# A Conformer/Hyena block on one NeuronCore: short convolutions in the tokens' own order, pieces turned by ScalarE, and the last group's LayerNorm laid beside its last short convolution

## The chip, the core and the metric

The kernel runs on one core of a Trainium2 chip. The metric is the time of one execution on the device, in microseconds; the kernel before takes 2048.83 us (median of three runs, 2046.94 to 2049.76). The engines are PE (TensorE, matrix products), DVE (VectorE), ACT (ScalarE), POOL (GpSimd; here it issues some transfers) and SP, which issues most transfers. Each works through its own instructions in order. "Column" below means 128 of the 7168 output channels of the input projection.

## What is computed

One encoder layer on 2048 tokens of width 1024 in float32: an RMSNorm, one input projection to 7168 channels, two mixers, and an output projection. The channels of both mixers come in eight groups of 128.

```python
p = einsum('bld,de->ble', rmsnorm(x), w_in)
c_val, c_gate, c_z, hy_p, hy_z = split(p)
a = c_val * sigmoid(c_gate)
a = depthwise_conv_centred(a, conf_dw_w)                 # width 31: 31 taps
a = silu(group_layernorm(a)) * silu(c_z)                 # 8 groups
hp = depthwise_conv_centred(hy_p, hy_short_w)            # width 3
x0, x1, v = split(hp)
y = bidir_fftconv(v * x1, h_fwd, h_bwd, hy_skip) * x0    # as a two-step transform
y = group_rmsnorm(y) * silu(hy_z)
out = rmsnorm(x + concat([a, y]) @ w_out)
```

## The kernel before

A column of the projection is computed in four *chunks* of 512 tokens (`chunk`, lines 242 to 251): for each of the eight 128-row blocks of the input three 512-wide matmuls (lines 246 to 248, since both operands are split into a high and a low part), so 24 matmuls a chunk. The result `mm` lies in one of four PSUM buffers until ACT or DVE has taken it. `fetch` (233 to 240) loads a column's weights and splits them: the high part `wh` by ACT (237), the low part `wl` by DVE (239). `wh` and `wl` have two buffers each, the raw `wr` one.

The middle of the kernel (from 340 us to 1465 us of the span) is a loop over the eight groups (694 to 735). In pass `i`:

- `conf_glu` forms gate times value of group `i` in `apad`, and the LayerNorm of group `i-1` (`conf_norm`) goes on meanwhile: ACT and DVE split each chunk of the sum `acc` (556, 557), two matmuls subtract the mean over the channels (562, 563), ACT squares and copies (564, 565), and four small matmuls form the variances (569). Then root, reciprocal (571, 572) and `stacked` (227 to 229).
- `conf_taps` adds the 31 taps of the width-31 convolution: each is one pass over 2048 tokens on DVE (541). It is a generator; `some(n)` issues the next `n` taps at the place in the program where it stands, so that DVE gets them between other work.
- `conf_tail` scales, gates and stores group `i-1` (584 to 590).
- `hz_gate` (only for `i` below 7) computes the gate's column.
- `hyena(i-1)`: `x1_out` and `gated` compute two columns; each chunk goes to `ppad` (608, ACT) and through `short_conv`: ACT multiplies by the middle weight (619), DVE adds the other two (621, 622). In `x1_out` the output is written *turned*: token 32 a + b lands at column 64 b + a of the tile (`turned`, 592 to 594), the order in which the transform wants it, so neighbours in time lie 64 elements apart. In `gated` the convolution is in the tokens' order, and DVE multiplies it into the turned tile (640).
- `stage1(i-1)`, the transform's first step, runs beside the chunks of `x0_out` (two of its steps in each chunk): PE transposes 512 columns of the gated tile (662), ACT takes the result (664), PE multiplies (679), ACT takes that (682) and SP stores it to `AU`. Transposes, products and the LayerNorm's matmuls share three PSUM buffers named `aux`.
- `x0_out` computes the third column, also turned (619, 621, 622), and `some(99)` issues all taps that are left.

After the loop come the three columns of group 7, with its LayerNorm and tail written between `hyena(7)` and `x0_out(7)`, the loads of the output weights (`wo_load`, by POOL) and their splits (`wo_split`), and the last gate's column (`hz_gate(7)`). Then the output projection starts (784 to 786) beside the transform's second step.

The program is not executed in exactly the order in which it is written: a scheduler puts each engine's instructions in order by the place in the program and by when it takes their inputs to be ready. The orders shown below are those that it put out.

The functions that the diff touches:

Of the kernel before, what the change touches and what calls it, by code (L numbers as in the profile page):

```python
# [13 lines left out]
AF = mybir.ActivationFunctionType  # L14
# [5 lines left out]
L = 2048  # L20
# [3 lines left out]
TC = 512  # L24
# [157 lines left out]
def hybrid_kernel(ctx: ExitStack, tc: tile.TileContext, A, out):  # L182
# [283 lines left out]
    def long(dt=F32):  # L466
        return wk.tile([P, L], dt, name="long", bufs=3)
# [30 lines left out]
    with ExitStack() as c0:  # L498
# [43 lines left out]
                                               op0=OP.mult, op1=OP.add)  # L542
                yield

        def conf_norm(prev):


            acc, = prev
            sqs, split = long(), None
            for t in range(NT + 1):  # L550
                ready = split
                if t < NT:
# [39 lines left out]
        def turned(x):  # L592

            return x.rearrange("p (n2 n1) -> p n1 n2", n2=N2)

        def hz_gate(i, some, store=True, order=range(NT)):
            hz = long()
            for t, ts, pt in inproj(48 + i, order=order):
                nc.scalar.activation(turned(hz)[:, 16 * t:16 * (t + 1)], pt.rearrange("p (a b) -> p a b", b=N2), AF.Copy)
                some(1)  # L600
            if store:
                nc.sync.dma_start(HZ[i], hz)
            return hz
# [6 lines left out]
                    after(t - 1)  # L610
            after(NT - 1)

        def short_conv(co, a, j, turn=False):
            n = TC

            def v(x):
                return x.rearrange("p (a b) -> p a b", b=N2) if turn else x

            nc.scalar.activation(co, v(ppad[:, a + 1:a + 1 + n]), AF.Identity, bias=sm("sh_b", j),  # L619
                                 scale=sm("sh_w", 3 * j + 1))  # L620
            nc.vector.scalar_tensor_tensor(co, v(ppad[:, a:a + n]), sm("sh_w", 3 * j), co, op0=OP.mult, op1=OP.add)  # L621
            nc.vector.scalar_tensor_tensor(co, v(ppad[:, a + 2:a + 2 + n]), sm("sh_w", 3 * j + 2), co,  # L622
                                           op0=OP.mult, op1=OP.add)

        def x1_out(i, some):
            s = long()

            def conv(t):
                short_conv(turned(s)[:, 16 * t:16 * (t + 1)], t * TC, 8 + i, turn=True)
                some(1)  # L630

            short_in(32 + i, after=conv)
            return s

        def gated(s, i, some):
            def conv(t):
                c = tmp()
                short_conv(c, t * TC, 16 + i)
                to = turned(s)[:, 16 * t:16 * (t + 1)]
                nc.vector.tensor_mul(to, to, c.rearrange("p (a b) -> p a b", b=N2))  # L640

            short_in(40 + i, after=conv)

        def x0_out(i, some, side, store=True):
            c = long()

            def conv(t):
                short_conv(turned(c)[:, 16 * t:16 * (t + 1)], t * TC, i, turn=True)
                some(1)

            short_in(24 + i, side, after=conv)
            if store:
                nc.sync.dma_start(X0[i], c)
            return c

        def stage1(i, s, some):
            def turn(q):
# [27 lines left out]
                yield  # L685

        def hyena(i, some):
            s = x1_out(i, some)
            gated(s, i, some)
            some(HY)  # L690
            return stage1(i, s, some)

        prev = side = None
        for i in range(NG):
# [22 lines left out]
            if i:  # L717
                side = hyena(i - 1, some)
                x0_out(i - 1, some, side)
            some(99)  # L720
        for _ in side:
            pass
        side = hyena(NG - 1, some)
        for _ in conf_norm(prev):
            pass
        wo_load(0, 0)
        conf_tail(NG - 1, *prev, lambda n: None)
        wo_split(0, 0, apad_tile(F32R))
        x0 = x0_out(NG - 1, lambda n: None, side, store=False)
        wo_load(0, 1, wp.tile([P, D], F32, name="wr", bufs=1))  # L730
        wo_load(0, 2, wp.tile([P, D], F32, name="wh"))
        wo_load(0, 3, wp.tile([P, D], F32, name="wl"))
# [375 lines left out]
```

## Time and profile before

| | us |
|---|---|
| median of three runs | 2048.83 |
| the profiled execution, whole | 2048.57 |
| its span, first to last instruction | 2046.8 |
| PE busy | 1981.5 (97%) |
| DVE busy | 1486.7 (73%) |
| ACT busy | 1046.6 (51%) |
| POOL busy | 44.2 (2%) |

The span is 1.8 us shorter than the execution. Matmuls are pipelined: each row of a 512-wide matmul has 0.39 us, but one starts every 0.23 us, so PE's busy time hides gaps shorter than a row. The granted clock is 1.00 where PE runs at its upper level (2.4 GHz) and 0.5 at its lower one (1.2 GHz).

### The profile page before, as it was taken

The page shows a single profiled execution, that of the slowest core. Times are in us where ns is not written, and L with a number is a line of the kernel's source. Part 1 is how long each engine was busy: PE and PEld are TensorE (multiplying, and loading weights), DVE is VectorE, ACT ScalarE, POOL GpSimd, SP SyncE. Part 2 cuts the span into 40 slices and gives each one's busy share as a digit, 9 for nine tenths or more (in the row PEclk, how much of TensorE's full clock was granted, in tenths as well). Part 3 has the DMA queues.
Part 4 walks back from the last instruction along what each step waited for, and adds up shares of the span by engine and source line. Part 5 has one row for each costly group of instructions (what it writes and reads, how often), then busy time and mean ns, then how long its engine had stood idle before and what let it go on. Part 6 is the DMA issues. An engine that isn't in the chain of part 4 may idle for free.

```text
span 2046.8 us, 23642 instructions
## 1 busy us (share of the span) xinstructions
PE 1981.5 (97%) x9304; PEld 1456.5 (71%) x9304; DVE 1486.7 (73%) x1339; ACT 1046.6 (51%) x1410; POOL 44.2 (2%) x90
## 2 busy tenths in 40 slices
PE   6999999999999999999999999999999999989998
PEld 4766688887787887887877877776655555556666
DVE  5587729499599599697795995997455555566774
ACT  5478711253343433433433534445677778555662
POOL 0000000000000000000000000000100000111110
PEclk9999999999999999999999999999999999999999
DMA  8524411120311212113202213121898888997862
GB/s 305 192 98 152 172 37 62 42 82 31 103 52 52 83 62 83 59 45 93 83 23 81 83 31 103 31 83 52 252 282 252 251 263 259 323 246 225 233 171 62
DMA packets 159663, 265.76 MB, mean 130 GB/s; under 512 B 12854, under 2 KB 99254, under 8 KB 155456
## 3 DMA queue, kind: packets, MB, share of 16 engines
q1 hardware_dynamic: 152448, 240.13, 38.0%
q0 software_dynamic: 7104, 24.12, 4.2%
q8 instruction: 73, 1.20, 0.3%
q14 instruction: 38, 0.31, 0.1%
HBM read 163.54 MB, written 100.66 MB: 129 GB/s over the span
## 4 chain that ended last, share of the span: by engine, by line
PE 71%; DVE 18%; issue 6%; ACT 3%; DMA 3%; POOL 0%; SPq 0%; DVEq 0%; POOLq 0%; ACTq 0%
PE mm L246 13%; PE mm L248 13%; PE mm L247 13%; DVE long L541 7%; PE o L784 6%; PE o L785 5%; PE o L786 5%; PE u L874 3%; PE k L874 3%; DVE long L622 2%; DVE long L621 2%; PE aux L679 1%; PE hp L382 1%; PE Y L971 1%; DVE t L622 1%
## 5 line engine op out<-in xcount | busy, mean ns | idle before, releaser
L246 PE MATMUL mm<-uh,wh 128*128 128x512 f32 x1792 | 710.3, 397 | 6.8 <-ACT wh L237 3.5
L248 PE MATMUL mm<-uh,wl 128*128 128x512 f32 x1792 | 702.4, 392 | 4.1 <-DVE wl L239 4.1
L247 PE MATMUL mm<-ul,wh 128*128 128x512 f32 x1792 | 702.3, 392 | 1.7 <-DVE ul L307 1.7
L541 DVE SCALAR_TENSOR_TENSOR long<-apad,small,long 128x2048 f32<-128x2048 f32 x240 | 564.5, 2352 | 8.9 <-ACT long L538 6.9
L246 PEld LDWEIGHTS mm<-uh,wh 128*128 128x128 f32 x1792 | 337.7, 189 | 107.3 <-issue 25.1
L248 PEld LDWEIGHTS mm<-uh,wl 128*128 128x128 f32 x1792 | 338.1, 189 | 78.5 <-DVE wl L239 5.1
L247 PEld LDWEIGHTS mm<-ul,wh 128*128 128x128 f32 x1792 | 338.3, 189 | 76.5 <-DVE ul L307 3.7
L608 ACT ACTIVATE ppad<-mm 128x512 f32<-128x512 f32 x96 | 57.3, 597 | 218.6 <-PE mm L248 196.6
L784 PE MATMUL o<-wo,mh 128*128 128x512 f32 x384 | 155.4, 405 | 1.5 <-ACT mh L1012 1.5
L786 PE MATMUL o<-wo,ml 128*128 128x512 f32 x384 | 152.4, 397 | 0.1
L785 PE MATMUL o<-wo,mh 128*128 128x512 f32 x384 | 152.5, 397 | 0.0
L883 ACT ACTIVATE long<-long 32x1024 f32<-32x1024 f32 x128 | 135.3, 1057 | 2.1
L237 ACT ACTIVATE wh<-wr 128x1024 fp32r<-128x1024 f32 x56 | 59.6, 1064 | 140.1 <-PE mm L247 129.8
L533 DVE TENSOR_TENSOR apad<-mm,apad 128x512 f32<-128x512 f32 x32 | 22.1, 691 | 147.4 <-PE mm L248 147.4
L889 DVE TENSOR_TENSOR long<-long,k 128x1024 f32<-128x1024 f32 x64 | 75.4, 1217 | 72.8 <-PE k L874 67.1
L784 PEld LDWEIGHTS o<-wo,mh 128*128 128x128 f32 x384 | 72.2, 188 | 46.2 <-issue 30.0
L239 DVE TENSOR_TENSOR wl<-wr,wh 128x1024 fp32r<-128x1024 f32 x56 | 68.6, 1225 | 41.7 <-ACT wh L237 41.0
L621 DVE SCALAR_TENSOR_TENSOR long<-ppad,small,long 128x512 f32<-128x512 f32 x64 | 85.8, 1343 | 6.5 <-ACT long L619 6.5
L619 ACT ACTIVATE long<-ppad,small 128x512 f32<-128x512 f32 x64 | 84.7, 1324 | 3.6 <-DMA HZ<-long 1.4
L622 DVE SCALAR_TENSOR_TENSOR long<-ppad,small,long 128x512 f32<-128x512 f32 x64 | 86.4, 1350 | 0.1
L786 PEld LDWEIGHTS o<-wo,ml 128*128 128x128 f32 x384 | 72.4, 189 | 17.5 <-issue 2.5
L785 PEld LDWEIGHTS o<-wo,mh 128*128 128x128 f32 x384 | 72.3, 188 | 17.7 <-issue 4.5
(176 smaller groups left out, 2294.5 us busy)
## 6 DMA issues: line engine op xcount, KB each, us to landing
wr<-in_w_in_dram SPq DMA_DIRECT2D x56, 512.0 KB, 3.6
AK<-ak SPq DMA_DIRECT2D x64, 256.0 KB, 2.0
AU<-t SPq DMA_DIRECT2D x64, 256.0 KB, 3.1
au<-AU SPq DMA_DIRECT2D x64, 256.0 KB, 4.3
ak<-AK SPq DMA_DIRECT2D x64, 256.0 KB, 5.2
VD<-vs SPq DMA_DIRECT2D x64, 256.0 KB, 4.4
long<-VD SPq DMA_DIRECT2D x16, 1024.0 KB, 7.5
xn<-in_x_dram SPq DMA_DIRECT2D x16, 512.0 KB, 5.7
```

Of the source, the lines that this page charges most:

```text
L246: mm(pt, wh[:, k], uh[t][:, k], start=(k == 0), stop=False)
L247: mm(pt, wh[:, k], ul[t][:, k], start=False, stop=False)
L248: mm(pt, wl[:, k], uh[t][:, k], start=False, stop=(k == KT - 1))
L541: nc.vector.scalar_tensor_tensor(acc, apad[:, j:j + L], sm("dw_w", i * CK + j), acc, op0=OP.mult, op1=OP.add)
L619: nc.scalar.activation(co, v(ppad[:, a + 1:a + 1 + n]), AF.Identity, bias=sm("sh_b", j), scale=sm("sh_w", 3 * j + 1))
L621: nc.vector.scalar_tensor_tensor(co, v(ppad[:, a:a + n]), sm("sh_w", 3 * j), co, op0=OP.mult, op1=OP.add)
L622: nc.vector.scalar_tensor_tensor(co, v(ppad[:, a + 2:a + 2 + n]), sm("sh_w", 3 * j + 2), co, op0=OP.mult, op1=OP.add)
L784: mm(o, mh[:, k], wh[:, cs], start=(k == 0), stop=False)
L785: mm(o, mh[:, k], wl[:, cs], start=False, stop=False)
L786: mm(o, ml[:, k], wh[:, cs], start=False, stop=(k == KT - 1))
L874: mm(o[rows2(k), HALF[i]], g[rows2(i), j:j + 64], x[rows2(i), HALF[k]], start=True, stop=True)
L883: nc.scalar.activation(uw[32 * q:32 * (q + 1)], us[32 * (q ^ 1):32 * (q ^ 1) + 32], AF.Copy)
```

## The change

Three things are changed.

1. `short_conv` works in the tokens' own order everywhere. Its turned accesses are gone; `turn_in` (622 to 623 in the changed file) lets ACT copy a finished piece into its turned place instead. `x1_out` turns nothing, `gated` multiplies into the small tile `c` and turns the product into a new long tile `g`, and `x0_out` turns its finished convolution. Per group that is eight turned copies on ACT more.
2. The taps of group 7 are no longer all issued before `hyena(7)`: `some(99)` stands behind it for the last group.
3. The LayerNorm of group 7 and its tail become a generator (`last_norm`) that takes one step each time `stage1(7)` takes one (`together`), that is two steps a chunk of `x0_out(7)`. Its squares lie in the tile of `apad` instead of a long one. The first load and split of output weights stand behind `x0_out(7)`.

```diff
-        def conf_norm(prev):
+        def conf_norm(prev, sqs=None):
...
-            sqs, split = long(), None
+            sqs, split = long() if sqs is None else sqs, None
...
-                nc.scalar.activation(turned(hz)[:, 16 * t:16 * (t + 1)], pt.rearrange("p (a b) -> p a b", b=N2), AF.Copy)
+                turn_in(hz, t, pt)
...
-        def short_conv(co, a, j, turn=False):
+        def short_conv(co, a, j):
             n = TC
-            def v(x):
-                return x.rearrange("p (a b) -> p a b", b=N2) if turn else x
-            nc.scalar.activation(co, v(ppad[:, a + 1:a + 1 + n]), AF.Identity, bias=sm("sh_b", j),
+            nc.scalar.activation(co, ppad[:, a + 1:a + 1 + n], AF.Identity, bias=sm("sh_b", j),
                                  scale=sm("sh_w", 3 * j + 1))
-            nc.vector.scalar_tensor_tensor(co, v(ppad[:, a:a + n]), sm("sh_w", 3 * j), co, op0=OP.mult, op1=OP.add)
-            nc.vector.scalar_tensor_tensor(co, v(ppad[:, a + 2:a + 2 + n]), sm("sh_w", 3 * j + 2), co,
+            nc.vector.scalar_tensor_tensor(co, ppad[:, a:a + n], sm("sh_w", 3 * j), co, op0=OP.mult, op1=OP.add)
+            nc.vector.scalar_tensor_tensor(co, ppad[:, a + 2:a + 2 + n], sm("sh_w", 3 * j + 2), co,
                                            op0=OP.mult, op1=OP.add)
+        def turn_in(to, t, x):
+            nc.scalar.activation(turned(to)[:, 16 * t:16 * (t + 1)], x.rearrange("p (a b) -> p a b", b=N2), AF.Copy)
 
         def x1_out(i, some):
             s = long()
             def conv(t):
-                short_conv(turned(s)[:, 16 * t:16 * (t + 1)], t * TC, 8 + i, turn=True)
+                short_conv(s[:, t * TC:(t + 1) * TC], t * TC, 8 + i)
                 some(1)
...
         def gated(s, i, some):
+            g = long()
             def conv(t):
                 c = tmp()
                 short_conv(c, t * TC, 16 + i)
-                to = turned(s)[:, 16 * t:16 * (t + 1)]
-                nc.vector.tensor_mul(to, to, c.rearrange("p (a b) -> p a b", b=N2))
+                nc.vector.tensor_mul(c, s[:, t * TC:(t + 1) * TC], c)
+                turn_in(g, t, c)
             short_in(40 + i, after=conv)
+            return g
 
         def x0_out(i, some, side, store=True):
-            c = long()
+            g = long()
             def conv(t):
-                short_conv(turned(c)[:, 16 * t:16 * (t + 1)], t * TC, i, turn=True)
+                c = tmp()
+                short_conv(c, t * TC, i)
+                turn_in(g, t, c)
                 some(1)
...
         def hyena(i, some):
-            s = x1_out(i, some)
-            gated(s, i, some)
+            s = gated(x1_out(i, some), i, some)
...
-            some(99)
+            if i < NG - 1:
+                some(99)
         for _ in side:
             pass
         side = hyena(NG - 1, some)
-        for _ in conf_norm(prev):
-            pass
+        some(99)
+
+        def last_norm():
+            yield from conf_norm(prev, apad_tile()[:, :L])
+            conf_tail(NG - 1, *prev, lambda n: None)
+            yield
+
+        def together(*steps):
+            live = list(steps)
+            while live:
+                for g in list(live):
+                    if next(g, live) is live:
+                        live.remove(g)
+                yield
+
+        side = together(last_norm(), side)
+        x0 = x0_out(NG - 1, lambda n: None, side, store=False)
         wo_load(0, 0)
-        conf_tail(NG - 1, *prev, lambda n: None)
         wo_split(0, 0, apad_tile(F32R))
-        x0 = x0_out(NG - 1, lambda n: None, side, store=False)
```

Three places of the engines' orders, before and after. In the changed file line 621 is 617, 622 is 618, 619 is 615, 640 is 641, 662 is 667, 664 is 669, 679 is 684 and 682 is 687; 623 is the turned copy.

The first is ACT, in a steady group (behind the third variance root, 571): the last piece of `gated` and the first ones of `x0_out`. Before:

```order
L237 ACTIVATE wh<-wr 128x1024
L608 ACTIVATE ppad<-mm 128x512
L619 ACTIVATE t<-ppad,small 128x512
L608 ACTIVATE ppad<-mm 128x512
L619 ACTIVATE long<-ppad,small 128x16x32
L608 ACTIVATE ppad<-mm 128x512
L619 ACTIVATE long<-ppad,small 128x16x32
L664 ACTIVATE t<-aux 128x512 x2
```

After:

```order
L237 ACTIVATE wh<-wr 128x1024
L608 ACTIVATE ppad<-mm 128x512
L615 ACTIVATE t<-ppad,small 128x512
L623 ACTIVATE long<-t 128x16x32
L608 ACTIVATE ppad<-mm 128x512
L615 ACTIVATE t<-ppad,small 128x512
L623 ACTIVATE long<-t 128x16x32
L608 ACTIVATE ppad<-mm 128x512
L623 ACTIVATE long<-t 128x16x32
L669 ACTIVATE t<-aux 128x512 x2
```

The turned copies (623) stand between the evacuation of a chunk (608) and the next; each waits for DVE's product, and the transposes' evacuation (669) stands behind the last of them.

The second is DVE in group 7, from the last taps to the LayerNorm's split (557). Before:

```order
L541 SCALAR_TENSOR_TENSOR long<-apad,small,long 128x2048
L622 SCALAR_TENSOR_TENSOR long<-ppad,small,long 128x16x32
L239 TENSOR_TENSOR wl<-wr,wh 128x1024
L621 SCALAR_TENSOR_TENSOR t<-ppad,small,t 128x512
L622 SCALAR_TENSOR_TENSOR t<-ppad,small,t 128x512
L640 TENSOR_TENSOR long<-long,t 128x16x32
L621 SCALAR_TENSOR_TENSOR t<-ppad,small,t 128x512
L622 SCALAR_TENSOR_TENSOR t<-ppad,small,t 128x512
L640 TENSOR_TENSOR long<-long,t 128x16x32
L621 SCALAR_TENSOR_TENSOR t<-ppad,small,t 128x512
L239 TENSOR_TENSOR wl<-wr,wh 128x1024
```

After:

```order
L239 TENSOR_TENSOR wl<-wr,wh 128x1024
L618 SCALAR_TENSOR_TENSOR long<-ppad,small,long 128x512
L541 SCALAR_TENSOR_TENSOR long<-apad,small,long 128x2048
L617 SCALAR_TENSOR_TENSOR t<-ppad,small,t 128x512
L541 SCALAR_TENSOR_TENSOR long<-apad,small,long 128x2048
L618 SCALAR_TENSOR_TENSOR t<-ppad,small,t 128x512
L641 TENSOR_TENSOR t<-long,t 128x512
L617 SCALAR_TENSOR_TENSOR t<-ppad,small,t 128x512
L618 SCALAR_TENSOR_TENSOR t<-ppad,small,t 128x512
L641 TENSOR_TENSOR t<-long,t 128x512
L617 SCALAR_TENSOR_TENSOR t<-ppad,small,t 128x512
L239 TENSOR_TENSOR wl<-wr,wh 128x1024
```

The first row of before is the last tap (541): it stood before all pieces of `gated`, and now the last one stands behind the first pass of the first piece. The next column's weight split (239, the second one in each) stands between two pieces, as before.

The third is PE in group 7's LayerNorm. Before:

```order
L563 MATMUL aux<-t,ctr 128x512
L562 MATMUL aux<-t,ctr 128x512
L248 MATMUL mm<-uh_95,wl 128x512
L246 MATMUL mm<-uh_100,wh 128x512
L247 MATMUL mm<-ul_101,wh 128x512
L563 MATMUL aux<-t,ctr 128x512
L569 MATMUL vp<-long,ones_g 32x512
L562 MATMUL aux<-t,ctr 128x512
L569 MATMUL vp<-long,ones_g 32x512
L248 MATMUL mm<-uh_100,wl 128x512
L563 MATMUL aux<-t,ctr 128x512
```

After, at the last two of the mean:

```order
L247 MATMUL mm<-ul_106,wh 128x512
L248 MATMUL mm<-uh_105,wl 128x512
L562 MATMUL aux<-t,ctr 128x512
L563 MATMUL aux<-t,ctr 128x512
L667 MATMUL aux<-ident,long 128x128 x4
L246 MATMUL mm<-uh_105,wh 128x512
```

and seven matmuls on:

```order
L248 MATMUL mm<-uh_105,wl 128x512
L246 MATMUL mm<-uh_105,wh 128x512
L247 MATMUL mm<-ul_106,wh 128x512
L248 MATMUL mm<-uh_105,wl 128x512
L569 MATMUL vp<-apad,ones_g 32x512 x4
L246 MATMUL mm<-uh_105,wh 128x512
```

Before, the four variance matmuls (569) were scattered among the mean's matmuls (562, 563) of the later chunks; now all four stand together, half a chunk behind the last of these, and a first transpose (667) stands between.

## Rows read from the trace of the kernel before

**Rows 1.** The page: busy time, share of the span, instructions per engine.

```profile
PE 1981.5 (97%) x9304; PEld 1456.5 (71%) x9304; DVE 1486.7 (73%) x1339; ACT 1046.6 (51%) x1410; POOL 44.2 (2%) x90
```

**Rows 2.** Waits of PE, 440 to 1260 us: who, for whom, total, times, longest.

```profile
PE aux L662 <- DVE long L640: 6.6, 6, 2.2
```

**Rows 3.** PE timeline: start us, us, line, operation, tiles [idle before, releaser].

```profile
492.13 0.66 PE L662 MATMUL aux<-ident,long 128*128 128x128 f32 x4 [0.83 <-DVE long L640]
...
1269.58 1.07 PE L569 MATMUL vp<-long,ones_g 128*32 128x512 f32 x8
...
1319.66 0.50 PE L248 MATMUL mm<-uh,wl 128*128 128x512 f32 x1 [3.80 <-DVE wl L239]
...
1400.35 0.50 PE L562 MATMUL aux<-t,ctr 128*128 128x512 f32 x1 [2.67 <-ACT t L556]
...
1404.92 0.50 PE L563 MATMUL aux<-t,ctr 128*128 128x512 f32 x1 [1.79 <-DVE t L557]
...
1407.42 1.92 PE L569 MATMUL vp<-long,ones_g 128*32 128x512 f32 x2
...
1441.61 1.12 PE L679 MATMUL aux<-t,st 64*128 64x512 f32 x2 [1.30 <-ACT t L682]
...
1464.81 0.39 PE L784 MATMUL o<-apad,mh 128*128 128x512 f32 x1
```

**Rows 4.** Windows: start:end length, busy us (count) per engine, granted clock, DMA share, GB/s.

```profile
1315.86:1351.46 35.60, 31.49 (x129) 22.47 (x129) 35.60 (x28) 17.56 (x25) 0.00 (x0) 0.95 0.21 63
1351.46:1397.68 46.22, 46.22 (x204) 37.91 (x202) 45.94 (x30) 13.64 (x17) 0.00 (x0) 1.00 0.20 66
1397.68:1464.81 67.13, 60.40 (x231) 41.00 (x232) 40.67 (x48) 43.42 (x68) 7.65 (x14) 0.95 0.49 160
```

**Rows 5.** Groups by line and shape: busy us, mean ns, idle before, releaser.

```profile
L621 DVE SCALAR_TENSOR_TENSOR long<-ppad,small,long 128x512 f32<-128x512 f32 x64 | 85.8, 1343 | 6.5 <-ACT long L619 6.5
L619 ACT ACTIVATE long<-ppad,small 128x512 f32<-128x512 f32 x64 | 84.7, 1324 | 3.6 <-DMA HZ<-long 1.4 <-ACT ppad L608 0.3
...
L608 ACT ACTIVATE ppad<-mm 128x512 f32<-128x512 f32 x96 | 57.3, 597 | 218.6 <-PE mm L248 196.6 <-DVE long L621 15.9 <-DVE wl L239 3.5
...
L640 DVE TENSOR_TENSOR long<-long,t 128x512 f32<-128x512 f32 x32 | 40.2, 1266 | 0.1
...
L599 ACT ACTIVATE long<-mm 128x512 f32<-128x512 f32 x32 | 35.3, 1104 | 43.6 <-PE mm L248 43.4
...
L619 ACT ACTIVATE t<-ppad,small 128x512 f32<-128x512 f32 x32 | 26.2, 820 | 1.1
...
L621 DVE SCALAR_TENSOR_TENSOR t<-ppad,small,t 128x512 f32<-128x512 f32 x32 | 24.0, 758 | 0.0
...
L588 DVE TENSOR_TENSOR long<-long,t 128x512 f32<-128x512 f32 x32 | 21.1, 681 | 0.2 <-ACT long L587 0.2
```

**Rows 6.** DVE timeline, columns as in Rows 3.

```profile
490.87 1.21 DVE L640 TENSOR_TENSOR long<-long,t 128x512 f32<-128x512 f32 x1
...
1318.33 1.28 DVE L239 TENSOR_TENSOR wl<-wr,wh 128x1024 fp32r<-128x1024 f32 x1
...
1389.07 2.33 DVE L541 SCALAR_TENSOR_TENSOR long<-apad,small,long 128x2048 f32<-128x2048 f32 x1
```

**Rows 7.** ACT timeline, columns as in Rows 3.

```profile
483.86 0.60 ACT L608 ACTIVATE ppad<-mm 128x512 f32<-128x512 f32 x1 [3.27 <-PE mm L248]
...
1399.68 1.14 ACT L556 ACTIVATE t<-long 128x512 fp32r<-128x512 f32 x2
...
1425.69 1.28 ACT L582 ACT_TABLE_LOAD   x1
1426.98 0.63 ACT L582 ACTIVATE t<-t 128x512 f32<-128x512 f32 x1
1427.52 0.80 ACT L587 ACTIVATE long<-long,small 128x512 f32<-128x512 f32 x1
```

**Rows 8.** Timeline of POOL, which issues output-weight loads, columns as in Rows 3.

```profile
1453.76 0.54 POOL L481 DMA_DIRECT2D t<-in_w_out_dram  x1 [3.16 <-ACT wo L494]
```

More of the change, by code (lines that the diff above doesn't have):

```diff
@@ L652, in x0_out @@
             if store:
-                nc.sync.dma_start(X0[i], c)
-            return c
+                nc.sync.dma_start(X0[i], g)
+            return g
         def stage1(i, s, some):
```

## The prediction

> **What bounds the kernel now.** I read the page first: PE is busy for 1981.5 of 2046.8 us [rows 1], and the change neither adds nor removes a matmul, so it can only give back time in which PE stands still or runs slowly, or add such time. Where that is I took from the waits of PE and from the busy time in windows of 20 us. The steady groups (440 to 1260 us) lose almost nothing: PE waits 6.6 us in six places, each time for DVE's gated product (640) before the first transposes [rows 2]; the first such place is shown [rows 3]. Most of the rest in reach lies in the last stretch of the middle, from 1315.86 us, where PE first stops, to 1464.81 us, where the output projection starts [rows 3]. In that stretch DVE is busy for all or nearly all of the first 82 us [rows 4].
>
> The ledger of that stretch: a matmul starts every 46.22 / 204 = 0.2266 us where nothing disturbs it [rows 4]. The stretch holds five columns of 96 less two: 478 x 0.2266 = 108.3 us. Two first steps of the transform take 6.2 us each where PE doesn't wait (my estimate: four transposes less than 0.45 each, eight products about 0.55), the LayerNorm's eight mean matmuls and four selections 0.23 each, the four variances 1.07 when they stand together [rows 3]: 16.2 us. Work is thus 124.5 of 148.95 us, and 24.4 us are lost. Rows name these: 3.80 us for the low weights (239) at 1319.66, 2.67 and 1.79 us for the LayerNorm's split, 1.30 us for a product's evacuation [rows 3]; the granted clock of 0.95 in two windows means 0.05 x (35.60 + 67.13) = 5.1 us at the cost of the lower level [rows 4]; the scattered variances, of which one pair takes 1.92 us against 1.07 for all four together [rows 3], cost about 3 us beside the clock's part. The rest, some 7 us, is in gaps between the products, where nothing else stood in PE's queue.
>
> **Removed from DVE.** A turned pass of `short_conv` takes 1.343 us, one in the tokens' order 0.758; the turned product 1.266, a plain one of the same shape 0.681 [rows 5]. I take line 622 like 621. Per group sixteen passes and four products: 16 x 0.585 + 4 x 0.585 = 11.7 us, 94 us over eight groups. It is worth only what PE waits for.
>
> **Added to ACT.** Eight bias passes get cheaper, 8 x (1.324 - 0.820) = 4.0 us [rows 5]. Eight turned copies come in, a form that the trace doesn't have: the turned copy from PSUM takes 1.104 and the turned bias pass from SBUF 1.324 us, and these are my bounds; I take 1.1, the copy being the nearer operation [rows 5]. ACT gets 8.8 - 4.0 = 4.8 us more per group (6.6 at the upper bound). It has room: it is busy for 17.6 of 35.6 and 13.6 of 46.2 us in the two windows that DVE fills [rows 4]. The room isn't the question, the order is (below).
>
> Here the Trainium skill has a rule, in "SBUF — State Buffer", section "Door 1: The DMA port swizzle": accesses that leave a 16-byte line at every element pay for it. The trace agrees (1.343 against 0.758 us). The same rule makes ACT's turned write slow, 1.104 against 0.597 us for a copy of the same size from PSUM to `ppad` [rows 5]: it moves the penalty rather than ending it, once per piece instead of on every pass.
>
> **Steady groups.** Up to the last gated product DVE saves eight passes and four products, 12 x 0.585 = 7.0 us. In the first group that product ended at 490.87 + 1.21 = 492.08 us [rows 6], now at about 485.1. ACT must still evacuate the next chunk at 483.86 [rows 7] and do its bias pass, until about 485.3, then turn the last piece: 486.4 (486.6 at the upper bound). PE wants it at 492.13 - 0.83 = 491.30 us [rows 3]. So the wait goes, with 4.9 us to spare: -6.6 us over the six groups.
>
> **First stall (group 6's columns).** The weights' split that PE waits for starts at 1318.33 us [rows 6], behind eight turned passes of `x1_out(6)`. These save 8 x 0.585 = 4.7 us, so it ends at about 1314.9 instead of 1319.6; PE needs it at 1319.66 - 3.80 = 1315.86 [rows 3]. The 3.80 us go, and with them the lower clock behind the stall, 0.05 x 35.60 = 1.8 us. The margin is 0.95 us. What is late next: the evacuations of `stage1(6)` on ACT now stand behind turned copies that wait for DVE's passes over `x0`. Walking both queues in their new order with the durations above I find PE held up by 1.3 us there.
>
> **LayerNorm of group 7.** The last tap starts at 1389.07 us [rows 6], and the first split (556) at 1399.68 [rows 7]. On the same walk DVE is through with `x0_out(6)` at 1344.9 and has eleven taps of 2.27 us, nine passes of 0.66 and two weight splits of 1.14 (single rows less the overlap with the next one) up to the last tap, which ends at about 1378; both columns before cost it 9.4 us less. The split is then bound by something else: ACT's weight copy for the last column, which waits until PE has finished `gated(7)`, at about 1388, stands before it. The split ends at 1391.0; PE, which has 208 matmuls from 1345.5 on until then (47.1 us), asks for it at 1392.7, and for the low part at 1393.3, some 0.3 us before DVE has it. So 2.67 + 1.79 us shrink to 0.3. The variances stand together again (3 us back), the reciprocal's chain ends at about 1414.3 us, and PE needs it at 1415.8.
>
> **First step of group 7.** Here a new wait takes the place of the old one. Once the chain is through, ACT has a table load of 1.28 us and four pairs of 0.63 and 0.80 us [rows 7], and then transposes' evacuations, bias passes, turned copies and products' evacuations, all in one queue. Three `aux` buffers are all PE has. The walk gives waits of 2.2 and 1.8 us at the third and fourth pair of products, against 1.30 us and the gaps around it before. I put one more spell of the lower clock behind them, 2.0 us, like that of 1.8 behind the first stall.
>
> **Taps, tile, loads.** The taps' place costs nothing: DVE still finishes them 10 us before the split can start. The squares' tile frees a long tile that `x0_out(7)` would have waited for, counted with the above. The output weights' loads go behind `x0_out(7)`: the last was issued at 1453.76 us [rows 8], 11 us before the projection; on the walk the last is issued at about 1438.5, some 10 us before it. ACT and DVE must still split each. I take 1.0 us for a late one; the bounds are 0 and 6 us.
>
> **The sum.** Left in the stretch: 1.3 + 0.3 + 4.0 + 2.0 + 1.0 = 8.6 us, so 24.4 - 8.6 = 15.8 us come back there and 6.6 in the steady groups, 22.4 us in all. From the profiled execution: 2048.57 - 22.4 = 2026.2 us; the median of the runs is 0.26 us above it, so I say 2026.5 us. What follows, the second step and the output projection, moves earlier as a whole: its first loads are released by PE's last chunks, as before.
>
> **Rivals.**
> - *Pile-up on ACT in the last group.* Only the steady 6.6 and the first stall's 5.6 us come back. For it: ACT's queue above is long, and any of its waits holds all behind it. Against: PE has 54 matmuls (12 us) left after the last product. 2048.8 - 12.2 = 2036.6 us.
> - *All clean.* No wait is left: 24.4 + 6.6 = 31.0 us, 2017.8 us. Against: four turned copies must stand somewhere between the evacuations.
> - *The waits weren't DVE's.* The named releaser is the one that came last; if the last stretch is bound by weight columns and transfers, only 6.6 us go: 2042.2 us. Against: DVE is busy for 81.5 of the 81.8 us before 1397.68 [rows 4].
> - *Slower: ACT's queue stops PE in every steady group.* Four turned copies stand between evacuations in `gated`, each waiting for DVE. If DVE stays as late as now and each of the four adds its 1.1 to 1.3 us to the next piece, the last copy ends at 492.08 + 5 = 497 us and PE waits 5.8 us a group instead of 0.9: 7 x 4.9 = 34 us, less the 15.8: 2067 us. It decides from the point where the last copy ends after 495.0 us in the first group, 3.7 us late; then 7 x (3.7 - 0.9) outweighs the stretch's gain by 4 us. Against: 486.4 on my walk.
>
> The Trainium skill speaks for this last one, in "TensorE: Matmul & The Clock Gate", section "Architectural detail: the array is 16× 32×32, not 1× 128×128": ACT and DVE take their instructions strictly in the order queued. The trace agrees: the LayerNorm's split (556) had its input at 1391.40 us and started at 1399.68, behind other work in ACT's queue [rows 6, 7].
>
> **How the numbers follow.** 0.2% of the time, 4.1 us, is about what a measurement can tell from no change. Forecast (2020 to 2032.5 us) 0.59; pile-up 0.17; clean 0.10; not DVE's 0.08, half of it within 4.1 us; slower 0.06. Faster: 0.59 + 0.17 + 0.10 + 0.04 = 0.90; same 0.04; slower 0.06. The range from 2017 to 2039 us holds the forecast, the pile-up and most of the clean case; beyond it lie the last two, 0.14, and some of the clean one.
>
> **What would show it.** Lines 617 and 618 at 0.76 us in all places, 641 at 0.68, the turned copies between 1.10 and 1.32; no wait of PE at the first transposes (667) in the steady groups; no wait for 239 and a clock of 1.00 behind `gated(6)`; the last tap ending before the last column's weight copy; the four variances in one row of about 1.1 us; waits at the products (684) of `stage1(7)` for ACT (687, 669). I am wrong if waits at 667 remain, if a wait for DVE stands before the LayerNorm's matmuls, or if the output projection starts less than 10 us earlier than at 1464.81.

## The result and the profile after

The changed kernel takes 2022.56 us (median of four runs, 2019.85 to 2027.15) against 2048.57 us for the kernel before (2048.83 is the median of the first three of its four runs); the ratio is 0.9876 with a 95% interval of 0.9856 to 0.9895. Measured again beside other kernels it took 2024.23 us against 2047.61, ratio 0.989 (0.9871 to 0.991). The forecast was 2026.5 us, with 2020 to 2032.5 for its own case and 2017 to 2039 as the whole range: faster, by 23 to 26 us where 22.4 were worked out. The profiled execution took 2022.32 us, its span 2020.6, 26.2 less than before.

I cut the span at three instructions that every kernel here has: the first variance matmul (569) of group 0 and of group 6, and the start of the output projection. "Steady" is from the first to the second, "end of the middle" from there to the projection, "last stage" the rest. The four columns are worked out from those starts and the span; the kernels of the experiments, told of below, stand here too.

| profiled execution | up to group 0 | steady | end of the middle | last stage |
|---|---|---|---|---|
| before | 410.8 | 858.78 | 195.23 | 582.0 |
| changed | 408.2 | 850.73 | 177.08 | 584.6 |
| changed, measured again | 411.0 | 850.71 | 176.92 | 582.7 |
| part 1 alone (e1) | 411.3 | 850.74 | 180.08 | 579.9 |
| parts 2 and 3 alone (e2) | 409.0 | 858.63 | 191.56 | 580.7 |
| without part 2 (e3) | 410.9 | 850.72 | 176.85 | 586.7 |
| copies by DVE (e4) | 411.0 | 850.52 | 177.59 | 584.0 |
| 3 copies more (e6_copies_3) | 409.8 | 850.72 | 176.75 | 585.4 |
| 8 copies more (e6_copies_8) | 409.3 | 892.10 | 184.20 | 586.0 |
| DVE writes turned (e9) | 409.2 | 850.51 | 177.67 | 586.9 |
| reciprocal first (e5) | 409.3 | 850.75 | 176.85 | 586.8 |
| sums later (e7) | 410.5 | 850.72 | 177.20 | 580.0 |
| e9 and e7 together (e10) | 410.5 | 850.52 | 177.40 | 583.8 |

The middle two columns hardly scatter from kernel to kernel with the same edit there (within 1 us); the first and the last scatter by 3 and 7 us. So 8.05 us came back in the steady groups and 18.15 at the end of the middle. That the changed kernel's profile starts 2.64 us earlier and ends 2.64 us worse is scatter: the second profile of the same kernel has 411.0 and 582.7.

The page's row of busy time, as in [rows 1]: DVE has 90.0 us less, ACT 32.3 more.

```profile
PE 1969.9 (97%) x9304; PEld 1454.1 (72%) x9304; DVE 1396.7 (69%) x1339; ACT 1078.9 (53%) x1474; POOL 44.2 (2%) x90
```

The waits of PE from 340 us to the start of the projection (who, for whom, total, times, longest), where [rows 2] had 6.6 us for DVE:

```profile
PE aux L684 <- ACT t L687: 1.1, 2, 0.6
PE o L802 <- ACT mh L768: 0.7, 1, 0.7
PE aux L684 <- ACT t L669: 0.4, 1, 0.4
```

Up to the projection no wait for DVE is left. PE's timeline at the places of [rows 3]: the first transposes of a steady group, the LayerNorm of group 7, its variances, the products of the last first step, the projection.

```profile
488.51 0.60 PE L667 MATMUL aux<-ident,long 128*128 128x128 f32 x4
...
1258.89 1.06 PE L569 MATMUL vp<-long,ones_g 128*32 128x512 f32 x8
...
1332.46 2.93 PE L684 MATMUL aux<-t,st 64*128 64x512 f32 x8 [0.50 <-ACT t L687]
...
1382.62 0.40 PE L562 MATMUL aux<-t,ctr 128*128 128x512 f32 x1
...
1383.40 0.51 PE L563 MATMUL aux<-t,ctr 128*128 128x512 f32 x1
...
1396.19 1.07 PE L569 MATMUL vp<-apad,ones_g 128*32 128x512 f32 x8
...
1418.31 1.60 PE L684 MATMUL aux<-t,st 64*128 64x512 f32 x4 [0.63 <-ACT t L687]
...
1421.18 1.61 PE L684 MATMUL aux<-t,st 64*128 64x512 f32 x4 [0.36 <-ACT t L669]
...
1435.97 0.50 PE L802 MATMUL o<-apad,mh 128*128 128x512 f32 x1 [0.72 <-ACT mh L768]
```

The windows up to the projection, to be read beside [rows 4]. The granted clock is 1.00 throughout, where two windows had 0.95, and in the second DVE is busy for only 29.44 of 44 us.

```profile
1305.10:1351.00 45.90, 45.40 (x201) 34.48 (x200) 45.79 (x37) 25.44 (x37) 0.00 (x0) 1.00 0.34 103
1351.00:1395.00 44.00, 44.00 (x197) 36.09 (x196) 29.44 (x31) 24.14 (x36) 0.68 (x1) 1.00 0.15 49
1395.00:1435.97 40.97, 39.26 (x170) 27.52 (x168) 20.88 (x28) 29.75 (x47) 6.94 (x13) 1.00 0.66 212
```

The groups by line and shape, as in [rows 5]: passes at 749 ns, the product at 688, the turned copy (623) at 1152 ns, inside the bounds of 1104 and 1324.

```profile
L623 ACT ACTIVATE long<-t 128x512 f32<-128x512 f32 x64 | 72.2, 1152 | 65.1 <-DVE t L641 41.3 <-DVE t L618 23.8
...
L618 DVE SCALAR_TENSOR_TENSOR t<-ppad,small,t 128x512 f32<-128x512 f32 x64 | 47.2, 749 | 4.9 <-ACT ppad L608 4.8
...
L641 DVE TENSOR_TENSOR t<-long,t 128x512 f32<-128x512 f32 x32 | 21.8, 688 | 0.1
```

On DVE, the split that PE waited for in [rows 6], and the last tap:

```profile
1303.01 1.22 DVE L239 TENSOR_TENSOR wl<-wr,wh 128x1024 fp32r<-128x1024 f32 x1
...
1365.62 2.35 DVE L541 SCALAR_TENSOR_TENSOR long<-apad,small,long 128x2048 f32<-128x2048 f32 x1
```

On ACT, the last turned copy of a steady group, the LayerNorm's first split, and the table load of group 7's tail, as in [rows 7]:

```profile
482.58 1.15 ACT L623 ACTIVATE long<-t 128x512 f32<-128x512 f32 x1
...
1380.13 0.62 ACT L556 ACTIVATE t<-long 128x512 fp32r<-128x512 f32 x1
...
1404.27 1.28 ACT L582 ACT_TABLE_LOAD   x1
```

A window (columns as in [rows 4]) from that table load to the end of the last first step, in which ACT is busy for 18.20 of 18.43 us:

```profile
1404.27:1422.70 18.43, 17.43 (x72) 10.69 (x70) 10.93 (x17) 18.20 (x29) 4.18 (x8) 1.00 0.73 234
```

On POOL, the last load of output weights ahead of the projection, as in [rows 8]:

```profile
1432.63 0.54 POOL L481 DMA_DIRECT2D t<-in_w_out_dram  x1 [0.77 <-DMA AU<-t]
```

What held the LayerNorm's split (556) in the kernel before isn't in [rows 6] and [rows 7]: DVE's split of the weights (239), the load of the last column's weights that SP issued behind it, and ACT's weight copy (237), which stands ahead of 556 in ACT's queue.

```profile
1392.57 1.21 DVE L239 TENSOR_TENSOR wl<-wr,wh 128x1024 fp32r<-128x1024 f32 x1
...
1393.85 0.33 SPq L235 DMA_DIRECT2D wr<-in_w_in_dram  x1
...
1397.38 1.06 ACT L237 ACTIVATE wh<-wr 128x1024 fp32r<-128x1024 f32 x1 [6.60 <-DMA wr<-in_w_in_dram]
```

In the changed kernel the load is issued at 1362.19 us, and the copy waits for PE and no longer for the load:

```profile
1377.83 1.06 ACT L237 ACTIVATE wh<-wr 128x1024 fp32r<-128x1024 f32 x1 [1.94 <-PE mm L247]
```

Times of before and after differ by 10.69 us at group 6's variances (1269.58 and 1258.89); to compare later places I add that to the changed kernel's.

### The profile page after: what moved, and what is told of

It is laid out like the page before. It is cut to its first block, busy times and chain, and to the rows that moved or that the text cites. A ratio compares the mean times of both kernels' runs of the same rounds, so it can differ in the third digit from the quotient of the medians.

```text
span 2020.6 us, 23652 instructions
## 1 busy us (share of the span) xinstructions
PE 1969.9 (97%) x9304; PEld 1454.1 (72%) x9304; DVE 1396.7 (69%) x1339; ACT 1078.9 (53%) x1474; POOL 44.2 (2%) x90
## 4 chain that ended last, share of the span: by engine, by line
PE 92%; ACT 3%; DMA 3%; DVE 2%; issue 1%; SPq 0%; POOL 0%; DVEq 0%; ACTq 0%; POOLq 0%
PE mm L246 20%; PE mm L247 20%; PE mm L248 20%; PE o L802 6%; PE o L804 5%; PE o L803 5%; PE u L892 3%; PE k L892 3%; PE aux L684 2%; PE Y L989 1%; PE hp L382 1%; DMA row<-PT 1%; PE op L404 1%; PE aux L667 1%; PE op L405 1%
## 5 line engine op out<-in xcount | busy, mean ns | idle before, releaser
L623 ACT ACTIVATE long<-t 128x512 f32<-128x512 f32 x64 | 72.2, 1152 | 65.1 <-DVE t L641 41.3
L564 ACT ACTIVATE long<-aux 128x512 f32<-128x512 f32 x28 | 16.6, 592 | 96.3 <-PE aux L563 96.3
L892 PE MATMUL k<-ak,g 64*64 64x512 f32 x512 | 61.5, 590 | 0.0
```

The source lines that it names most:

```text
L623: nc.scalar.activation(turned(to)[:, 16 * t:16 * (t + 1)], x.rearrange("p (a b) -> p a b", b=N2), AF.Copy)
L892: mm(o[rows2(k), HALF[i]], g[rows2(i), j:j + 64], x[rows2(i), HALF[k]], start=True, stop=True)
```

## Experiments

**e1 and e2: the parts alone.** e1 is the changed kernel with the last group written as before; e2 is the kernel before with parts 2 and 3.

```diff
 e1, against the changed kernel:
-            if i < NG - 1:
-                some(99)
+            some(99)
...
-        some(99)
...
-        side = together(last_norm(), side)
-        x0 = x0_out(NG - 1, lambda n: None, side, store=False)
+        for _ in conf_norm(prev):
+            pass
         wo_load(0, 0)
+        conf_tail(NG - 1, *prev, lambda n: None)
         wo_split(0, 0, apad_tile(F32R))
+        x0 = x0_out(NG - 1, lambda n: None, side, store=False)
```

Expected of e1:

> Part 1 alone: convolutions in the tokens' order with turned copies on ACT; group 7's taps, LayerNorm and loads as before. My theory (DVE was late in the steady groups and at the first stall, the order of the last group is worth the rest): the steady groups give 8 us back and the first stall 5.6, so that 2035 us result (2031 to 2038); four variances still scattered, a LayerNorm split that still waits. Rival 1 (DVE relief is all that counts): as fast as the whole change, 2020 to 2025. Rival 2 (the order is what counts): 2040 or more.

Expected of e2:

> Parts 2 and 3 alone: group 7's taps spread, its LayerNorm in steps with the first step's; convolutions turned by DVE as before. My theory: the six steady waits (6.6 us) and the 3.80 us for the low weights remain, the variances stand together and the gaps in the last first step shrink, but DVE is late for the LayerNorm's split: 5 us back, 2043 us (2039 to 2047). Rival 1 (DVE relief is all that counts): 2047 to 2051. Rival 2 (the order is what counts): 2030 to 2036.

e1: 2026.37 us (2021.25 to 2028.2), ratio 0.9895 (0.988 to 0.991). e2: 2047.48 us, ratio 1.0003 (0.9993 to 1.0014). My figures were 2035 (2031 to 2038) and 2043 (2039 to 2047). Both missed on the side of rival 1: e2 lies in its range, e1 1.4 us above it. The waits of PE up to the projection, in e1:

```profile
PE aux L684 <- ACT t L687: 1.9, 4, 0.6
```

and in e2:

```profile
PE aux L662 <- DVE long L640: 6.4, 6, 2.0
PE aux L563 <- DVE t L557: 4.8, 1, 4.8
PE mm L248 <- DVE wl L239: 3.8, 1, 3.8
PE o L798 <- ACT mh L764: 1.8, 1, 1.8
PE aux L679 <- ACT t L682: 1.5, 2, 1.2
...
```

With the passes made cheap every wait for DVE is gone, the LayerNorm's too, though its order was not touched. With the order alone all of them stay; at the end of the middle e2 gains 3.67 us, but that gain can't be told from nothing in its time (the profiled execution, 2041.68 us, was the fastest of twelve). What e1 lacks there against the whole change is 3.0 us. Its variance matmuls still stand apart, four rows of 1.04 us instead of one of 1.07, which is 3.1 us (two of the four are shown):

```profile
1388.94 1.04 PE L569 MATMUL vp<-long,ones_g 128*32 128x512 f32 x2
...
1395.70 1.04 PE L569 MATMUL vp<-long,ones_g 128*32 128x512 f32 x2
```

**e3: without part 2.** The taps of group 7 are again all issued before `hyena(7)`.

```diff
-            if i < NG - 1:
-                some(99)
+            some(99)
...
         side = hyena(NG - 1, some)
-        some(99)
```

> The changed kernel with part 2 undone: all taps of group 7 issued before hyena(7) again. My theory: the taps' place costs nothing, as DVE ends them 12 us before the first split in the changed kernel: 2022.6 us, within 4 us of the changed kernel; at most the first stall of 3.80 us for the low weights comes back (2026). Rival (the spread taps are what frees DVE for the columns before): 2028 or more, with a wait of PE for 239 or for a product of DVE.

2023.45 us, ratio 0.9882 (0.9867 to 0.9897), with 176.85 us at the end of the middle and no wait for DVE: the taps' place is worth nothing that these times or this trace show.

**e4: the copies on DVE.** The edit changes the call in `gated` and in `x0_out`, eight copies a group; one of the two is shown.

```diff
+        def turn_dve(to, t, x):
+            nc.vector.tensor_copy(turned(to)[:, 16 * t:16 * (t + 1)], x.rearrange("p (a b) -> p a b", b=N2))
...
-                turn_in(g, t, c)
+                turn_dve(g, t, c)
```

> The changed kernel with the three columns' turned copies on DVE instead of ACT: DVE then has 8 copies of some 1.27 us (the turned product's row, an estimate) more a group and keeps 11.7 - 10.1 = 1.6 us of its relief. My theory (what comes back is DVE's relief, ACT's copies cost nothing): the steady waits go by a hair (last copy 1.1 us before PE asks), part of the first stall and of the LayerNorm's wait returns, 2035 us (2028 to 2042). Rival 1 (ACT's longer queue is what the changed kernel now pays for): faster than it, under 2021. Rival 2 (DVE must be relieved by the full 11.7 us): no gain, 2045 or more.

2022.03 us, ratio 0.9885 (0.987 to 0.9899): as the changed kernel, and in none of the ranges that I had written down. The reason is the price. Lines by shape, columns as in [rows 5]:

```profile
L627 DVE COPY long<-t 128x512 f32<-128x512 f32 x64 | 38.7, 629 | 0.1
```

The copy takes 0.63 us, half of my estimate and about half of what ACT needs. So DVE keeps 11.7 - 8 x 0.63 = 6.7 us of its relief per group, and that is enough. PE waits for no product of DVE up to the projection. Which engine copies decides nothing here.

**e6: how much room ACT has.** The last piece of `gated` is turned 3 or 8 more times in groups 0 to 6.

```diff
-                turn_in(g, t, c)
+                for _ in range(1 + 8 if t == NT - 1 and i < NG - 1 else 1):
+                    turn_in(g, t, c)
```

> The changed kernel with ACT turning the last piece of gated four times instead of once in groups 0 to 6 (same result, three copies of 1.15 us more a group). My theory: the last copy ends 4.8 us before PE's first transposes ask for it (483.73 against 488.51 us in the first group), so 3 x 1.07 = 3.2 us fit: no wait, 2022.6 us within 4. Rival (ACT's queue is already at its limit, any copy more delays PE): 7 x 3.2 = 22 us more, 2045.

> The same with eight copies more: six stand before the next chunk's evacuation (608), two behind it. My theory: the last copy ends at 483.73 + 8 x 1.07 + 0.5 = 492.8 us, 4.3 us after PE asks at 488.51; seven groups give 30 us, 2053 us (2045 to 2060), with a wait of some 4 us at 667 for ACT's copy in each. Rival (the margin is wider, since PE's queue has other work, or the evacuation's delay is hidden in four buffers): no wait, 2023 to 2027.

Three copies: 2023.51 us, ratio 0.9886 (0.9871 to 0.9901), and no wait in the steady groups. Eight: 2073.11 us, ratio 1.0132 (1.0117 to 1.0147), slower than before and above the 2045 to 2060 that I expected. ACT's timeline in the first group:

```profile
483.74 8.07 ACT L623 ACTIVATE long<-t 128x512 f32<-128x512 f32 x7
491.62 0.61 ACT L608 ACTIVATE ppad<-mm 128x512 f32<-128x512 f32 x1
492.14 3.12 ACT L623 ACTIVATE long<-t 128x512 f32<-128x512 f32 x3
```

and PE's:

```profile
494.39 1.11 PE L668 MATMUL aux<-ident,long 128*128 128x128 f32 x4 [4.57 <-ACT long L623]
...
496.16 0.63 PE L248 MATMUL mm<-uh,wl 128*128 128x512 f32 x1
496.58 0.63 PE L246 MATMUL mm<-uh,wh 128*128 128x512 f32 x1
```

The wait, 4.57 us, is what I had worked out (4.3), but a group costs 41.4 / 6 = 6.9 us in the mean. Windows behind the waits of the first and the second group (columns as in [rows 4]) show the rest: PE is granted the lower level, 1.2 GHz, and a matmul starts every 0.42 us instead of 0.23. In the first group that lasts for 3 us, and from one group's variances (569) to the next one's it takes 147.96 us, 6.2 more than the changed kernel's 141.75. In the second it lasts for 6.7 us, part of them still in the wait, and the group takes 7.2 us more. Three of the six groups are like the first (6.2 to 6.3 us) and three like the second (7.2 to 8.1).

```profile
494.40:497.40 3.00, 3.00 (x9) 2.56 (x10) 2.96 (x2) 1.45 (x2) 0.00 (x0) 0.50 0.03 5
497.40:505.00 7.60, 7.60 (x35) 5.45 (x34) 6.60 (x6) 3.15 (x6) 0.00 (x0) 1.00 0.00 0
640.90:647.60 6.70, 5.07 (x14) 4.20 (x15) 6.63 (x4) 3.06 (x4) 0.00 (x0) 0.50 0.01 2
```

**e9: DVE writes the turned place itself.** `short_conv`'s second pass over x0 and the product in `gated` read in the tokens' order and write turned; the columns' eight copies go. Two of its places (the pass's new lines in `short_conv` are left out):

```diff
-                nc.vector.tensor_mul(c, s[:, t * TC:(t + 1) * TC], c)
-                turn_in(g, t, c)
+                nc.vector.tensor_mul(turned(g)[:, 16 * t:16 * (t + 1)], v(s[:, t * TC:(t + 1) * TC]), v(c))
...
-                turn_in(g, t, c)
+                short_conv(c, t * TC, i, turned(g)[:, 16 * t:16 * (t + 1)])
```

> The changed kernel without the columns' turned copies: DVE's second pass over x0 and its product in gated read in the tokens' order and write the turned place themselves. Theory (what made DVE's turned passes slow was the turned read, not the turned write: the turned copy on DVE took 0.629 us, where the turned pass of before took 1.343): the pass takes 0.75 and the product 0.68 us with a turned output, ACT has 9.2 us less a group, and the time stays at 2022.6 us within 4, since PE waited neither for DVE nor for the copies. Rival (a turned write costs DVE too, as it costs ACT): 1.2 us or more for the pass and the product, 4.7 us of the relief gone in each group, and waits for DVE return in the last group: 2025 to 2032.

On the operation the rival was right. The time, 2026.11 us, ratio 0.9893 (0.9876 to 0.9909), lies in the theory's range and in the rival's, and can't be told from the changed kernel's 2024.23 on the same chip. The trace has one wait for DVE again, 0.2 us for the LayerNorm's low part (563), and the end of the middle takes 177.67 us against 176.92. The lines by shape, the pass written turned, the product written turned, the same pass written in order:

```profile
L619 DVE SCALAR_TENSOR_TENSOR long<-ppad,small,t 128x512 f32<-128x512 f32 x32 | 35.2, 1141 | 3.5 <-ACT ppad L608 3.5
L643 DVE TENSOR_TENSOR long<-long,t 128x512 f32<-128x512 f32 x32 | 34.3, 1084 | 0.1
...
L619 DVE SCALAR_TENSOR_TENSOR t<-ppad,small,t 128x512 f32<-128x512 f32 x32 | 23.6, 743 | 0.5 <-ACT ppad L608 0.5
```

In these two operations a turned output costs DVE 0.40 us, so e9 keeps 11.7 - 8 x 0.40 = 8.5 us of the relief (four passes and four products), again enough but for those 0.2 us.

**e5 and e7: the turn into the last stage.** The longest wait of the changed kernel's last stage is for the stacked reciprocal. PE's timeline in it, then DVE's:

```profile
1775.96 0.80 PE L1023 MATMUL R<-rs,sel 128*128 128x256 f32 x2 [10.05 <-DVE rs L229]
```

```profile
1770.67 1.23 DVE L1041 TENSOR_TENSOR row<-row,xr 128x1024 f32<-128x1024 f32 x1 [11.29 <-issue]
1771.81 1.75 DVE L1012 RECIPROCAL r<-r 128x256 f32<-128x256 f32 x1
...
1775.43 0.48 DVE L229 SCALAR_TENSOR_TENSOR rs<-rs,part,r 128x256 fp32r<-128x256 f32 x1
```

The reciprocal stands behind a sum that is held up. e5 puts it ahead by drawing its two lines into the part with a written order; e7 writes the sums later.

```diff
 e5:
-        m, vp = next(block)
-        st[1] = normed(1, m, deviations(vp))
+            m, vp = next(block)
+            st[1] = normed(1, m, deviations(vp))
 e7:
-        pts = {b: residual(b) for b in range(2)}
+        pts = {}
...
                 st[b + 2] = normed(b + 2, m, deviations(vp))
+                if b == 0:
+                    pts = {c: residual(c) for c in range(2)}
```

> The changed kernel with one more pair of lines in the part whose order is written out: the second block's reciprocal of the output's RMSNorm (1012) stands ahead of the residual sums (1041) on DVE. Theory: in the changed kernel the reciprocal stands behind a sum that waits 11.29 us for a load, and PE waits 10.05 us for its result; so PE's wait falls to under 2 us and some 6 to 10 us come back: 2014 us (2011 to 2018). Rival (PE is bound there by transfers anyway: the loads of the residual and of the transform come in at the same time): the wait moves to another line and the time stays within 4 us of 2022.6.

> The changed kernel with the first two residual sums written behind the third block's RMSNorm. Theory now (the turn into the last stage is bound by transfers, busy for 1.03 of 16 queues' time between 1755.97 and 1795.97 us): the wait of PE moves again, 2019 to 2026. Rival (the order of DVE's queue there sets it): 2010 to 2017.

e5: 2025.72 us, ratio 0.9896 (0.9883 to 0.991); e7: 2020.5 us, ratio 0.9874 (0.9857 to 0.989). Neither can be told from the changed kernel, so e5 missed its theory and fell to its rival, and e7 lies in its theory's range. PE's wait for the reciprocal is gone from e5's last stage; its longest waits are in other places:

```profile
PE T L996 <- ACT y L991: 6.8, 1, 6.8
PE vp L1005 <- ACT sq L1000: 3.9, 3, 3.0
...
```

This speaks for the reading that the turn is bound by its transfers, but no run took a transfer away, so that stays open.

**The changed kernel again, and e9 with e7's sums (e10).**

> The changed kernel once more, beside the next two on one chip. Expected within 4 us of 2022.6 us; in the profile 1.4 us or less of PE's waits between 340 us and the output projection for ACT (687, 669), none for DVE; from the output projection to the end between 580 and 587 us, as in the ten profiled executions so far, with a wait for the stacked reciprocal (229).

> The last one and the two residual sums written later, together: a version meant to beat both. From the two alone (nothing for the first, 2 us for the second by medians): 2018 to 2022 us. Rival (ACT's 9.2 us less a group also shorten the last first step's waits, some 2 us): 2016 to 2019.

The changed kernel came as expected, but for PE's waits at the products, 1.5 us where 1.4 were put down at most. Its times are told of above (584.6 and 582.7 us for the last stage, the wait for the reciprocal being 10.05 us in the one and 9.9 in the other, so that it doesn't explain the difference). e10: 2022.75 us, ratio 0.9877 (0.9859 to 0.9894), above the 2018 to 2022 that I expected. No version here beats the change by more than can be measured.

## Why the prediction was right, and where its sizes were off

- **Steady groups: right place, 6.6 us against 8.05.** All of it is part 1 (850.74 in e1, 858.63 in e2). The step that was mis-sized is reading the wait off the row. In [rows 3] the idle time before the transposes starts where the row of the last matmul ends, 0.39 us after its start, while the next one could have started after 0.23. So each wait costs 0.16 us more than the 0.83 shown, and the transposes behind it take 0.06 more (0.66 against 0.60): 6 x 0.22 = 1.3 us. The margin was met: the last turned copy ends at 482.58 + 1.15 = 483.73 us, PE asks at 488.51, 4.8 us to spare where 4.9 were worked out. e6 shows it from both sides: three copies more fit, eight don't.
- **First stall: right.** The split ends at 1304.23 us; PE asks at 1315.86 - 10.69 = 1305.17, 0.94 us later (predicted 0.95). The wait at the products behind it is listed with 0.50 us instead of 1.3; by the starts of the rows that first step lost 1.0 us (worked out under the sum).
- **LayerNorm of group 7: right in size, by DVE's relief, but on another way than I had read.** The last tap ends at 1378.7 on the clock of before (predicted about 1378), the first split at 1391.4 (1391.0). The 4.46 us went wholly, where I had left 0.3, though by a hair: DVE's low part ends at 1383.35 us and PE takes it at 1383.40. What I had not seen is how DVE held the split in the kernel before. The last tap was through at 1391.40 us, and the split (556) stood for 8.3 us more behind ACT's weight copy (237), which waited 6.60 us for its load; that load was issued at 1393.85, when DVE's split of the weights (239) had ended at 1393.78 and released the one raw buffer `wr` (SP had waited 28.2 us for it). So PE's 2.67 us were not for the taps but for DVE's place in the weights' chain; the 1.79 us behind them were for DVE's own half of the split (557). In the changed kernel that weight split starts at 1360.89 us, 21 us earlier on the clock of before, and in e1, by the cheaper passes alone, 16 us earlier. In e2 the weight copy doesn't wait for its load either, and PE waits 4.8 us for 557. My expectation for e1 forgot what this walk said: by e1 these waits go without the order, and by e2 the order alone doesn't end them. Of part 3 the runs show that the variances stand together, 3.0 us, as put down (e1 against the changed kernel, part 2 being worth nothing by e3).
- **First step of group 7: right engine, wrong size.** ACT is busy almost without a gap from the table load at 1404.27 us on, and PE waits for it at the third and fourth pair of products, as put down, but 0.63 + 0.36 = 0.99 us in place of 4.0 (2.5 us by the starts of the rows, worked out under the sum), and the spell of the lower clock (2.0 us) didn't come: the granted clock stayed at 1.00. This is the largest miss of the sum. In the trace 17, 10 and 3 chunks' matmuls stand between the four pairs of products, and PE works through them while ACT catches up. Why the walk gave PE longer waits stays open, since its rows aren't on record.
- **Taps: right** (e3). **Output weights: right size, other cause.** PE waits 0.72 us before the projection's first matmul (1.0 put down) and 0.53 us two matmuls on, for the mixer's own operands (768, 770) and not for a weight, though the last load is issued at 1443.3 us on the clock of before, 4.8 later than on the walk.
- **The sum.** Lost in the stretch after the change: 130.80 (1305.17 to 1435.97) - 124.5 = 6.3 us, where 8.6 were left. So 18.15 came back instead of 15.8, and with the steady groups 26.2 instead of 22.4. In the stretch two errors ran against each other. My 6.2 us for a first step of the transform without a wait are too low: in each steady group of the changed kernel, from the first transposes to the first matmul behind the last products (488.51 to 514.43 us in the first), 84 of the chunks' matmuls stand, and 25.93 - 84 x 0.2266 = 6.9 us are left. The kernel before has 7.0 there, so its trace could have told me. So 1.4 us of what I called lost was work, and 4.9 of the 6.3 us are still lost. In the same way the first step of group 6 took 17.85 - 44 x 0.2266 = 7.9 us, and that of group 7 29.81 - 81 x 0.2266 = 11.45, of which the variances and the selections (584) took 2.04: 1.0 and 2.5 us lost, where 1.3 and 6.0 were put down. That the sum for the stretch is off by 2.3 us and not by 3.7 (18.15 - (24.4 - 1.4 - 8.6)) is luck.
- **The rivals.** Pile-up on ACT fell, since no wait for DVE is left and those for ACT sum to 1.5 us. That the waits weren't DVE's fell by e1 and e2. The slower one was a true mechanism that needs more delay than there is: e6 made it happen with eight copies, and then the kernel is 1.3% slower than before. Its price per group was too low, since it counted the wait without the lower clock behind it. "All clean" (31.0 us) was the nearest rival; 6.3 of its 24.4 us in the stretch are still lost (4.9 of 23.0 with the first steps as measured).
- **Where I read the trace too far.** I told ACT's turned copy and DVE's turned passes by one rule of the Trainium skill ("SBUF — State Buffer", section "Door 1: The DMA port swizzle": accesses that leave a 16-byte line at every element pay). The runs agree that there is a price, not that it is one price: on DVE a pass with turned input and output took 1.343 us, with a turned output 1.141, with none 0.743, and a plain copy with a turned output 0.629. The nearest copy in order, `row<-o` from PSUM (842), takes 0.689 there, so no price of turning shows in the copy; no run has the same copy from SBUF in order.

## What to carry to other kernels

Where one engine is busy without a gap before each wait of another, make its instructions cheaper before moving them: here 6.7 us a group off DVE removed every wait for it, and the new order on its own none. Before you name what holds an instruction, read what stands ahead of it in its engine's queue and what that waits for: the LayerNorm's split stood behind a weight load, not behind the taps. Price a new queue on another engine by the end of its last instruction against the time at which it is asked for (4.8 us here), not by its busy time, and read the granted clock behind a stall, as it is part of the price: 4.6 us of waiting cost 6.2 to 7.2 us here. Measure work between the starts of rows, since listed waits leave part of a gap out: 0.99 us listed were 2.5. A profile's first and last stages can scatter by more than the edit is worth; cut the span at instructions that both kernels have and compare the pieces.

## What the runs showed that I had not expected

- DVE's turned copy (0.629 us for 128 x 512) costs about half of ACT's (1.152), and less than a pass in the tokens' order (0.749).
- A stop of PE of 4.57 us was followed by 3 us at the lower level in e6's first group, where it cost 6.2 us, and by more in others. The length of one stop doesn't tell whether that comes: the longest stop of the steady groups before, 2.2 us [rows 2], had a granted clock of 1.00 behind it (779.00 to 786.00 us), while in the last first step before, behind a stop of 1.30 us at 1441.61 [rows 3] with shorter ones ahead of it, there is a window at 0.50:

```profile
1443.60:1446.90 3.30, 3.30 (x10) 2.53 (x9) 0.00 (x0) 0.00 (x0) 2.10 (x4) 0.50 0.96 336
```

- DVE's relief per group was 11.7 us in the changed kernel, 8.5 in e9 and 6.7 in e4, by the rows' durations (90.0, 71.4 and 63.1 us over all groups by the pages' busy time), and the stages of the middle are the same within 0.8 us: once the last wait is gone, more relief is worth nothing.
